# Scores of all attention heads as 64-row products, and the first gate and up weight splits pinned behind the heads, in a two-layer hybrid decoder trunk

## Chip, core and metric

One core of a Trainium2 chip runs the whole program. The metric is the time of one execution in microseconds; the kernel before has a median of 1226.44 us over three runs. Engines are named as in the profile: PE is the matrix engine (PEld its weight loads), DVE, ACT and POOL are the vector, scalar and GpSimd engines, SP issues most of the transfers.

## What is computed

Two layers, each on 512 tokens of width 1024, all in float32. The first half of a layer mixes tokens with two groups of heads; the second half is a gated feed-forward network (hidden width 2816). Cut to what matters:

```python
h = rms_norm(x, attn_pre_g[l]); proj = h @ w_in[l]
# 4 differential heads: two score maps of 64 features each, rotary on a quarter of them
logits = einsum('bqhmd,bkhmd->bhmqk', qi, k) * scale           # m = 0, 1
p = softmax(where(causal, logits, NEG_INF)); p = p[:, :, 0] - lam * p[:, :, 1]
oa = rms_norm(einsum('bhqk,bkhe->bqhe', p, v), diff_sub_g[l]) * (1.0 - lam_init)
# 8 forgetting heads: one score map of 64 features, and a bias from cumulated log gates
logits = einsum('bqhd,bkhd->bhqk', qi, k) * scale + decay
ob = einsum('bhqk,bkhd->bqhd', softmax(where(causal, logits, NEG_INF)), v)
x = x + rms_norm(concat(oa, ob) @ w_out[l], attn_post_g[l])
h = rms_norm(x, ffn_pre_g[l])
x = x + rms_norm((silu(h @ w_gate[l]) * (h @ w_up[l])) @ w_down[l], ffn_post_g[l])
```

## The kernel before

Every float32 operand is split into a high and a low part of a reduced type (a cast on ACT, then a subtraction on DVE or POOL), and a product is the sum of three products: high by high, low by high, high by low. `hT_h` and `hT_l` hold the normed activations, transposed, in the two parts; a weight tile comes through `load_w` (L255) into a raw buffer `wr` and is split into `wh` and `wl`.

**Order.** The head part of a layer (projections, 12 heads, most of the output projection) is written as operations with durations, dependences and slots (`Plan`, L58). The planner walks a simulated clock and emits the instructions of each engine in the order that it finds; `keep_in_program_order` then pins them. PE's fillers are the projections `pj_kd`, `pj_qd`, `pj_kf`, `pj_qf` and the values `vb`, in steps of three products, later the output projection `o`; scores, transposes and value products of the heads go between them. What is not pinned (`load_w` of the feed-forward part) is placed by the framework's scheduler, which may put it among the pinned instructions of ACT and DVE. Each engine works strictly in the order so found.

**Scores.** `tile_chunk` (L693) makes the queries (`q`) or keys (`k`) of 128 features: two maps of a differential head, or two forgetting heads. Its function `stack` gives each of the two 64-feature halves its own full-height operand of 128 rows: for queries the high part in 64 rows and the low part in the other 64; for keys, per half, a high tile and a low tile, each written into 64 rows and then copied to the other 64 by a transfer (`dup`, L742). With 128 rows a single product then sums two of the three terms, so `score` (L880) needs two products per block: stacked queries by the high keys, and by the low keys. Scores land in PSUM banks of tag `s`, of which there are two (`bank_s`). `i` counts the four blocks of 128 queries; block `i` needs `(i+1)*128` key columns. Names in the profile: `sd` and `sf` are the score banks of differential and forgetting heads, `qsd`, `ksd`, `qsf`, `ksf` the operands, `ptd` and `ptf` the transposed probabilities, `od` and `of` the value products, `mixf` the mixed outputs, `pq` a small transpose of the cumulated gates.

**First feed-forward weights.** `gate(0)`, `up(0)` and `gate(f1)` (L1257 and L1260, through `proj_T`) are called after the heads, and their splits are not pinned.

Of the kernel before, what the change touches and what calls it, by code (L numbers as in the profile page):

```python
# [11 lines left out]
F32 = mybir.dt.float32  # L12
# [5 lines left out]
P = 128  # L18
S = 512
# [51 lines left out]
class Plan:  # L71
# [112 lines left out]
def hymba_block(ctx, tc, x_d, pos_d, apre_d, win_d, fb_d, lq1_d, lk1_d, lq2_d, lk2_d, dsg_d, wout_d, apost_d,  # L184
# [67 lines left out]
    G.memset(halfpi, math.pi / 2)  # L252


    def load_w(src, shape, name, eng=None, dst=None, raw=None):  # L255
        n = int(np.prod(shape[1:]))

        def t(tag, dt):
            w = wpool.tile([P, WCH], dt, name=f"{tag}_{name}", tag=tag)[:, :n]
            return w.rearrange("p (a b) -> p a b", a=shape[1])  # L260
        if raw is None:
            w = wpool.tile([P, WCH], F32, name=f"wr_{name}", tag="wr", bufs=NRAW)[:, :n]
            raw = w.rearrange("p (a b) -> p a b", a=shape[1])
        hi, lo = dst or (t("wh", F32R), t("wl", F32R))
        nc.sync.dma_start(raw, src)
        A.copy(hi, raw)  # L266
        (eng or V).tensor_sub(lo, raw, hi.bitcast(F32))  # L267
        return hi, lo

    def split(hi, lo, src):  # L270
# [54 lines left out]
            if store:  # L325
                nc.sync.dma_start(out_d[t * P:(t + 1) * P, c], xs[:, t, c])

    def proj_T(src_w, col, name):

        wh, wl = load_w(src_w[:, col:col + P].rearrange("(k p) n -> p k n", p=P), [P, KT, P], name)  # L330
        ps = bank_g(f"pj_{name}")

        def part(c=slice(0, S), ks=range(KT)):
            for k in ks:
                mm(ps[:, c], wh[:, k], hT_h[:, k, c], k == 0, False)
                mm(ps[:, c], wh[:, k], hT_l[:, k, c], False, False)
                mm(ps[:, c], wl[:, k], hT_h[:, k, c], False, k == KT - 1)
        return ps, part
# [16 lines left out]
    for l in range(DEPTH):  # L355
        win = win_d[l]
        with ExitStack() as actx:
# [339 lines left out]
            def tile_chunk(kind, z, which):  # L697

                need = 8 * z if kind == "d" else 32 + 8 * z
                col = {"dq": QA, "dk": KA, "fq": QB, "fk": KB}[kind + which] + z * P  # L700
                name = f"{which}{kind}{l}{z}"
                box, ready = load(win[:, col:col + P].rearrange("(k p) n -> p k n", p=P), [P, KT, P], name,
                                  eng=V if kind == "d" and l == z == 0 else G)
                b = {}

                def piece(k):
                    def fn():
                        if k == 0:
                            b["ps"] = bank_g(f"pj_{name}")
                        w = box["w"]  # L710
                        mm(b["ps"], w[0][:, k], hT_h[:, k], k == 0, False)
                        mm(b["ps"], w[0][:, k], hT_l[:, k], False, False)
                        mm(b["ps"], w[1][:, k], hT_h[:, k], False, k == KT - 1)
                    return fn
                last_tile[:] = fillers([(650, piece(k)) for k in range(KT)], [ready], take={0: ["g"]}, give=["w"],
                                       key=FILLER - 40 if kind == "d" and l == z == 0 else FILLER)
                done = last_tile[-1]
                key = need - AHEAD_T
                tag = "qs" if which == "q" else "ks"

                def stack(src, deps, give, eng):
                    E = {"V": V, "G": G}[eng]

                    def hi(m):
                        def fn():
                            if m == 0:
                                b["x"] = (q_tile if which == "q" else k_tile)(f"{which}s{kind}{z}")
                            r = HALF[m]
                            return A.copy(b["x"][r, m] if which == "q" else b["x"][r, m, 0], src()[r])
                        return fn  # L730

                    def lo(m):
                        def fn():
                            r, o = HALF[m], HALF[1 - m]
                            x = b["x"]
                            if which == "q":
                                return E.tensor_sub(x[o, m], src()[r], x[r, m].bitcast(F32))
                            return E.tensor_sub(x[r, m, 1], src()[r], x[r, m, 0].bitcast(F32))
                        return fn

                    def dup(m):
                        return lambda: nc.sync.dma_start(b["x"][HALF[1 - m], m].bitcast(F32),  # L742
                                                         b["x"][HALF[m], m].bitcast(F32))
                    ends = []
                    for m in range(2):
                        a = add("A", dA(S), hi(m), deps, key=key, take=[] if m else [tag], order="" if m else tag)
                        d = dV(S) if eng == "V" else dG(S)
                        e = add(eng, d, lo(m), [a], key=key, give=give if m else [], port=kind == "d")
                        if which == "k":
                            e = add("Q", 730, dup(m), [e], key=key, lat=2000)  # L750
                        ends.append(e)
                    qk[(kind, z, which)] = (b, ends)

                if kind == "f":
                    stack(lambda: b["ps"], [done], ["g"], "V")
# [19 lines left out]
                stack(lambda: b["t1"], [g1], ["rc"], "V")  # L775

            vf, vdone = {}, {}
            c_dram = dpool.tile([NFOX, S], F32, name=f"cdram{l}", tag="cdram")
# [102 lines left out]
            def score(kind, h, i, m, n_key, bias=None, pair=None):  # L881
# [8 lines left out]

                def mms():
                    b["s"] = bank_s(f"s{name}")
                    q, ks = qb["x"][:, half, i * P:n], kb["x"]
                    mm(b["s"][:, :n], q, ks[:, half, 0, :n], True, False)
                    mm(b["s"][:, :n], q, ks[:, half, 1, :n], False, True)

                def top():
                    if bias:
# [16 lines left out]
                give = []  # L915
                if i == NT - 1 and (m == 1 if kind == "d" else h % 2):
                    give = ["qs", "ks"]
                o = add("P", n / 1.2 + 5 + PEX / 2, mms, q_ends + k_ends + st["score"] + (bias["op"] if bias else []),
                        key=n_key, take=["s"] if bias else ["s", "e"], give=give)
                st["score"] = [o]  # L920
                v = add("V", dV(n)+80, top, [o], key=n_key, give=["s"])
                return b, add("A", 370 + 0.87 * n, expo, [v], key=n_key)

            def probs(kind, h, i, e_of, deps, key):

# [40 lines left out]
            def diff_head(h, n0):  # L966
                hd = heads.setdefault(("d", h), {"T": []})
                for i in range(NT):
                    n = (i + 1) * P
                    l2 = {}  # L970
                    x = [score("d", h, i, m, n0 + 2 * i + m, pair=l2) for m in range(2)]
                    key = n0 + 2 * i + 1
                    b = {}

# [212 lines left out]
            o1_chunks()  # L1187
            cv = [conv(k, 100) for k in (6, 7)]
            plan.run(tc.keep_in_program_order, first)

            def o0_last(t):
                for k in (6, 7):
# [33 lines left out]
        with ExitStack() as fctx:  # L1226
# [28 lines left out]
                    nc.sync.dma_start(t_d[x, f * P:(f + 1) * P], t)  # L1255

            def gate(f):  # L1257
                return proj_T(wg_d[l], f * P, f"g{l}{f}")

            def up(f):  # L1260
                return proj_T(wu_d[l], f * P, f"u{l}{f}")

            first = {}

# [207 lines left out]
```

## Time and profile before

| what | value |
|---|---|
| median of three runs (lowest, highest) | 1226.44 us (1226.29, 1489.4) |
| the profiled execution, its own time | 1230.15 us |
| its span in the trace | 1228.4 us |
| PE busy, PEld busy | 97 %, 81 % of the span |
| DVE, ACT, POOL busy | 66 %, 49 %, 16 % |
| mean granted clock of PE | 0.987 |

Busy time of an engine is the union of its instructions. PE's products overlap, so a step is read from one start to the next. The page divides the span into 40 slices of 30.7 us; slices 2 to 8 and 21 to 28 hold the head parts of the two layers. The chain of work that ended last is 86 % PE.

### The profile page before, as it was taken

How to read it: one execution, taken by the hardware profiler on the slowest of the kernel's cores; microseconds unless marked ns; L12 is line 12 of the kernel's file. 1: busy time of each engine (PE TensorE's matmuls, PEld its weight loads, DVE VectorE, ACT ScalarE, POOL GpSimd, SP SyncE). 2: the span in 40 equal slices, each digit the busy share in tenths (PEclk: the TensorE clock that was granted, in tenths of full speed). 3: DMA queues.
4: the chain of work that ended last, by engine and by line, in shares of the span. 5: the costliest groups of instructions: out<-in, count | busy, mean ns of one | idle time of the engine just before them, and what ended most of it. 6: DMA issues, size and time to landing. Idle time of an engine off the chain costs nothing.

```text
span 1228.4 us, 16747 instructions
## 1 busy us (share of the span) xinstructions
PE 1196.9 (97%) x5826; PEld 995.6 (81%) x5826; DVE 808.9 (66%) x1588; ACT 598.4 (49%) x1164; POOL 198.6 (16%) x243
## 2 busy tenths in 40 slices
PE   8999999999999999999999899998999999999997
PEld 5888988798888888888778789876988888888886
DVE  6788868565555545577839777784655555455776
ACT  6467767453233232465535768663532332324653
POOL 1213456120000000000231215560200000000010
PEclk9999999999999999999999899998999999999999
DMA  6334444216766757798413333442167667677964
GB/s 217 95 96 117 108 121 136 88 53 201 223 210 208 230 183 234 242 306 301 129 52 89 101 86 88 130 146 69 53 201 225 208 205 230 186 241 235 315 232 138
DMA packets 210884, 206.54 MB, mean 168 GB/s; under 512 B 11360, under 2 KB 155360, under 8 KB 210800
## 3 DMA queue, kind: packets, MB, share of 16 engines
q1 hardware_dynamic: 210128, 204.95, 53.5%
q8 instruction: 46, 0.75, 0.3%
q10 hardware_dynamic: 672, 0.53, 0.1%
q14 instruction: 38, 0.31, 0.1%
HBM read 163.20 MB, written 33.85 MB: 160 GB/s over the span
## 4 chain that ended last, share of the span: by engine, by line
PE 86%; issue 5%; DVE 4%; POOL 2%; DMA 1%; ACT 1%; POOLq 0%; DVEq 0%; SPq 0%
PE pj_g L214 20%; PE pj_u L214 20%; PE o L214 5%; PE da L214 5%; PE dc L214 5%; PE pj_kd L214 4%; PE vb L214 4%; PE pj_qd L214 4%; PE pj_kf L214 4%; PE pj_qf L214 3%; PE va L214 3%; PE db L214 2%; PE sd L214 2%; PE of L214 1%; PE od L214 1%
## 5 line engine op out<-in xcount | busy, mean ns | idle before, releaser
L214 PE MATMUL pj_g<-hT_h,wh_g 128*128 128x512 f32 (+1 forms) x384 | 142.9, 372 | 0.0
L214 PE MATMUL pj_g<-hT_l,wh_g 128*128 128x512 f32 (+1 forms) x384 | 142.7, 372 | 0.0
L214 PE MATMUL pj_g<-hT_h,wl_g 128*128 128x512 f32 (+1 forms) x384 | 142.6, 371 | 0.0
L214 PE MATMUL pj_u<-hT_h,wh_u 128*128 128x512 f32 (+1 forms) x368 | 140.1, 381 | 0.0
L214 PE MATMUL pj_u<-hT_l,wh_u 128*128 128x512 f32 (+1 forms) x368 | 139.8, 380 | 0.0
L214 PE MATMUL pj_u<-hT_h,wl_u 128*128 128x512 f32 (+1 forms) x368 | 139.7, 380 | 0.0
L266 ACT CAST wh_g<-wr_g 128x1024 fp32r<-128x1024 f32 x44 | 46.4, 1054 | 153.1 <-PE pj_u L214 92.3
L267 DVE TENSOR_TENSOR wl_u<-wr_u,wh_u 128x1024 fp32r<-128x1024 f32 x44 | 53.9, 1225 | 94.5 <-ACT wh_u L266 94.5
L279 POOL TENSOR_SCALAR v_fp<-s_fp 128x1 f32<-128x1 f32 x8 | 7.6, 946 | 664.1 <-DVE c L1398 624.9
L266 ACT CAST wh_u<-wr_u 128x1024 fp32r<-128x1024 f32 x44 | 46.3, 1052 | 133.2 <-PE pj_g L214 128.8
L1268 DVE TENSOR_TENSOR sg<-pj_u,sg 128x512 f32<-128x512 f32 x44 | 30.4, 691 | 85.6 <-PE pj_u L214 85.6
L214 PEld LDWEIGHTS pj_g<-hT_h,wh_g 128*128 128x128 f32 x384 | 72.4, 188 | 12.7
L214 PE MATMUL da<-wh_d,op 128*128 128x512 f32 x264 | 82.6, 390 | 0.0
L214 PEld LDWEIGHTS pj_g<-hT_h,wl_g 128*128 128x128 f32 x384 | 72.2, 188 | 12.5
L214 PEld LDWEIGHTS pj_g<-hT_l,wh_g 128*128 128x128 f32 x384 | 72.3, 188 | 12.4
L214 PEld LDWEIGHTS pj_u<-hT_h,wl_u 128*128 128x128 f32 x368 | 69.2, 188 | 13.1
L214 PEld LDWEIGHTS pj_u<-hT_h,wh_u 128*128 128x128 f32 x368 | 69.1, 188 | 13.1
L214 PEld LDWEIGHTS pj_u<-hT_l,wh_u 128*128 128x128 f32 x368 | 69.2, 188 | 12.9
L266 ACT CAST wh_d<-wr_d 128x1024 fp32r<-128x1024 f32 x42 | 44.2, 1052 | 43.3 <-PE da L214 10.7
L267 DVE TENSOR_TENSOR wl_d<-wr_d,wh_d 128x1024 fp32r<-128x1024 f32 x42 | 51.3, 1220 | 15.3 <-ACT wh_d L266 15.2
L266 ACT CAST wh_d<-xr 128x1024 fp32r<-128x1024 f32 (+1 forms) x42 | 38.2, 908 | 42.2 <-PE da L214 12.5
L214 PEld LDWEIGHTS da<-wh_d,op 128*128 128x128 f32 x264 | 49.6, 188 | 10.3
(293 smaller groups left out, 3089.2 us busy)
## 6 DMA issues: line engine op xcount, KB each, us to landing
wr_g<-in_w_gate_dram SPq DMA_DIRECT2D x44, 512.0 KB, 4.5
wr_u<-in_w_up_dram SPq DMA_DIRECT2D x44, 512.0 KB, 4.1
b<-in_w_down_dram SPq DMA_DIRECT2D x88, 256.0 KB, 3.6
t_d<-b SPq DMA_DIRECT2D x88, 256.0 KB, 4.2
wr_d<-t_d SPq DMA_DIRECT2D x24, 512.0 KB, 4.8
wr_d<-in_w_down_dram SPq DMA_DIRECT2D x18, 512.0 KB, 5.0
wr_o<-in_w_out_dram SPq DMA_DIRECT2D x16, 512.0 KB, 3.7
xr<-t_d SPq DMA_DIRECT2D x16, 512.0 KB, 5.1
```

What stands on the lines that cost most here:

```text
L214: ins = PE.matmul(out, a, b, start=start, stop=stop)
L266: A.copy(hi, raw)
L267: (eng or V).tensor_sub(lo, raw, hi.bitcast(F32))
L279: G.tensor_scalar(v, s2[:, 0:1], scalar1=s2[:, 1:2], scalar2=EPS, op0=ALU.add, op1=ALU.add)
L1268: V.tensor_mul(sg, pu, sg)
```

## The change

The high and low parts of queries and keys are no longer stacked into 128 rows. `parts_of` takes the place of `stack`: one cast and one subtraction over all 128 rows, into a high and a low tile; no copies. A score then multiplies 64 rows by 64 rows, in three products. For a differential head, `score_pair` emits the products of its two maps in turn, one on rows 0 to 63, the other on rows 64 to 127, with both `s` banks taken at once; a forgetting head emits its three products on one and the same half. The planner's durations for the scores follow. Apart from that, the splits of the first gate and the first up tile are called right behind the planned part and pinned there. The diff, cut:

```diff
-    def load_w(src, shape, name, eng=None, dst=None, raw=None):
+    def load_w(src, shape, name, eng=None, dst=None, raw=None, pin=False):
...
-        A.copy(hi, raw)
-        (eng or V).tensor_sub(lo, raw, hi.bitcast(F32))
+        for ins in (A.copy(hi, raw), (eng or V).tensor_sub(lo, raw, hi.bitcast(F32))):
+            if pin:
+                tc.keep_in_program_order(ins)
...
+    def feature_w(src_w, col, name, pin=False):
+        return load_w(src_w[:, col:col + P].rearrange("(k p) n -> p k n", p=P), [P, KT, P], name, pin=pin)
+
+    def proj_T(src_w, col, name, w=None):
+
+        wh, wl = w or feature_w(src_w, col, name)
...
-                def stack(src, deps, give, eng):
...
-                            return A.copy(b["x"][r, m] if which == "q" else b["x"][r, m, 0], src()[r])
...
-                            if which == "q":
-                                return E.tensor_sub(x[o, m], src()[r], x[r, m].bitcast(F32))
-                            return E.tensor_sub(x[r, m, 1], src()[r], x[r, m, 0].bitcast(F32))
...
-                        return lambda: nc.sync.dma_start(b["x"][HALF[1 - m], m].bitcast(F32),
-                                                         b["x"][HALF[m], m].bitcast(F32))
...
+                def parts_of(src, deps, give):
+
+                    def hi():
+                        x = (q_tile if which == "q" else k_tile)(f"{which}s{kind}{z}")
+                        b["x"] = x if which == "q" else x[:, 0]
+                        return A.copy(b["x"][:, 0], src())
+
+                    def lo():
+                        return V.tensor_sub(b["x"][:, 1], src(), b["x"][:, 0].bitcast(F32))
...
-                    q, ks = qb["x"][:, half, i * P:n], kb["x"]
-                    mm(b["s"][:, :n], q, ks[:, half, 0, :n], True, False)
-                    mm(b["s"][:, :n], q, ks[:, half, 1, :n], False, True)
+                    r = HALF[half]
+                    for y, (qx, kx) in enumerate(((0, 0), (0, 1), (1, 0))):
+                        mm(b["s"][:, :n], qb["x"][r, qx, i * P:n], kb["x"][r, kx, :n], y == 0, y == 2)
...
-                o = add("P", n / 1.2 + 5 + PEX / 2, mms, q_ends + k_ends + st["score"] + (bias["op"] if bias else []),
+                o = add("P", n / 0.8 + 8 + PEX / 2, mms, q_ends + k_ends + st["score"] + (bias["op"] if bias else []),
...
+            def score_pair(h, i, n_key, l2):
...
+                    for m in range(2):
+                        bs[m]["s"] = bank_s(f"sd{l}{h}{i}{m}")
+                    for z, (x, y) in enumerate(((0, 0), (0, 1), (1, 0))):
+                        for m, r in enumerate(HALF):
+                            mm(bs[m]["s"][:, :n], qb["x"][r, x, i * P:n], kb["x"][r, y, :n], z == 0, z == 2)
...
+                o = add("P", 1.3 * n + 60, mms, q_ends + k_ends + st["score"], key=n_key, take=["s", "s", "e", "e"],
+                        give=["qs", "ks"] if i == NT - 1 else [])
...
-                    x = [score("d", h, i, m, n0 + 2 * i + m, pair=l2) for m in range(2)]
+                    x = score_pair(h, i, n0 + 2 * i, l2)
...
             plan.run(tc.keep_in_program_order, first)
+            early = [feature_w(x[l], 0, f"{n}{l}0", True) for n, x in (("g", wg_d), ("u", wu_d))]
...
-                return proj_T(wg_d[l], f * P, f"g{l}{f}")
+                return proj_T(wg_d[l], f * P, f"g{l}{f}", None if f else early[0])
...
-                return proj_T(wu_d[l], f * P, f"u{l}{f}")
+                return proj_T(wu_d[l], f * P, f"u{l}{f}", None if f else early[1])
```

What PE does at the first scores of a forgetting head in layer 0: before, two products per block on 128 rows.

```order
L214 MATMUL vb_1549<-wh_vb_0_1325,hT_l 128x256
L214 MATMUL sd_1568<-ksd_0_1313,qsd_0_1394 128x512 x2
L219 MATMUL ptd_1573<-con,ed_1454 128x128 x2
L214 MATMUL sf_1576<-ksf_0_1425,qsf_0_1506 128x128 x2
L214 MATMUL vb_1549<-wh_vb_0_1325,hT_h 128x256
```

After the change, three on 64 rows; the blocks are still enclosed by 128-row work (`vb` are values, `ptd` transposes).

```order
L214 MATMUL vb_1560<-wh_vb_0_1361,hT_l 128x256
L214 MATMUL sf_1578<-ksf_0_1423,qsf_0_1511 128x128 x3
L214 MATMUL sf_1584<-ksf_0_1423,qsf_0_1511 128x256 x3
L219 MATMUL ptd_1595<-con,ed_1473 128x128 x2
L214 MATMUL vb_1560<-wh_vb_0_1361,hT_h 128x256
```

The width shown (128x256) is that of the result: queries by keys. Between 128-row products there now stand short runs of 64-row products.

At the first differential head PE had, per block, two products for each of the two maps (bank by bank), with filler steps around them.

```order
L214 MATMUL pj_kd_569<-hT_h,wl_kd_467 128x512
L214 MATMUL sd_592<-ksd_0_503,qsd_0_553 128x256 x2
L214 MATMUL sd_596<-ksd_0_503,qsd_0_553 128x256 x2
L214 MATMUL pj_kd_569<-hT_h,wh_kd_466 128x512
L214 MATMUL pj_kd_569<-hT_l,wh_kd_466 128x512
```

Now the products of a block alternate between the two banks, that is between rows 0 to 63 and rows 64 to 127.

```order
L214 MATMUL pj_kd_571<-hT_l,wh_kd_466 128x512
L214 MATMUL pj_kd_571<-hT_h,wl_kd_467 128x512
L214 MATMUL sd_588<-ksd_0_503,qsd_0_543 128x256
L214 MATMUL sd_589<-ksd_0_503,qsd_0_543 128x256
L214 MATMUL sd_588<-ksd_0_503,qsd_0_543 128x256
```

The alternation goes on to six products; then the filler returns. In the whole changed program the 384 score products stand in 81 such unbroken runs, 30 that begin with a differential head and 51 with a forgetting one.

On ACT, at the end of the heads of layer 0, the splits of the first gate and up tile stood among the exponentials (`ae`) and the casts of the probabilities (`pthf`).

```order
L914 ACTIVATE ae_2623,lf_2664<-ae_2623,mf_2658 128x256
L266 CAST wh_g_3067<-wr_g_3066 128x1024
L914 ACTIVATE ae_2635,lf_2682<-ae_2635,mf_2670 128x384
L1090 COPY mixf_1886<-of_2672 64x512
L947 CAST pthf_2692<-ptf_2694 128x128
L266 CAST wh_u_3074<-wr_u_3073 128x1024
L1098 CAST hT_h<-mixf_1886 128x512
```

Now both stand behind the last cast of the heads, ahead of the squares for the norm (`junk`).

```order
L971 CAST pthf_2747<-ptf_2793 128x384
L1114 COPY mixf_1904<-of_2811 64x512
L1122 CAST hT_h<-mixf_1904 128x512
L266 CAST wh_g_2847<-wr_g_2846 128x1024
L266 CAST wh_u_2853<-wr_u_2852 128x1024
L286 ACTIVATE junk_2869,s_ap_2868<-o_2438 128x512
```

No instruction of a head is queued behind them any more. On SP the transfers of the two raw tiles now stand ahead of those of the two gains of the norms (`g_apost`, `g_fpre`), where they stood behind them.

## Rows read from the trace of the kernel before

**Rows 1.** The page: busy time of engines, then the granted clock in 40 slices.

```profile
PE 1196.9 (97%) x5826; PEld 995.6 (81%) x5826; DVE 808.9 (66%) x1588; ACT 598.4 (49%) x1164; POOL 198.6 (16%) x243
...
PEclk9999999999999999999999899998999999999999
```

**Rows 2.** Windows of both head parts: length, busy (instructions) of PE, PEld, DVE, ACT, POOL, clock, DMA.

```profile
42.00:260.00 218.00, 214.78 (x1163) 180.61 (x1162) 171.06 (x447) 147.19 (x346) 82.23 (x95) 0.99 0.37 105
636.00:875.00 239.00, 225.36 (x1175) 188.47 (x1176) 177.97 (x455) 147.13 (x347) 82.45 (x97) 0.96 0.34 98
```

**Rows 3.** Windows at half clock within the head parts, same columns.

```profile
223.60:227.03 3.43, 3.43 (x12) 2.41 (x11) 2.61 (x7) 1.23 (x5) 0.00 (x0) 0.50 0.66 193
...
838.00:844.84 6.84, 5.99 (x17) 4.51 (x18) 3.07 (x8) 1.10 (x4) 0.00 (x0) 0.50 0.47 136
...
677.60:684.40 6.80, 5.81 (x22) 4.73 (x20) 6.70 (x19) 2.93 (x8) 0.00 (x0) 0.50 0.16 33
...
701.50:708.30 6.80, 6.18 (x17) 5.04 (x18) 4.03 (x15) 4.76 (x18) 0.00 (x0) 0.50 0.28 77
```

**Rows 4.** Timeline, ACT, both ends of heads: start, length, instruction, [idle before <-releaser].

```profile
219.47 1.05 ACT L266 CAST wh_g<-wr_g 128x1024 fp32r<-128x1024 f32 x1 [2.02 <-DMA wr_g<-in_w_gate_dram]
...
832.94 1.05 ACT L266 CAST wh_g<-wr_g 128x1024 fp32r<-128x1024 f32 x1 [3.42 <-DMA wr_g<-in_w_gate_dram]
```

**Rows 5.** Timeline, PE, at the same two places.

```profile
222.55 0.87 PE L219 MATMUL ptf<-con,ae 128*128 128x128 f32 x5 [1.80 <-DVE mixf L1092]
...
837.12 0.66 PE L219 MATMUL ptf<-con,ae 128*128 128x128 f32 x4 [3.56 <-DVE mixf L1092]
838.85 0.48 PE L219 MATMUL ptf<-con,ae 128*128 128x128 f32 x1 [1.07 <-DVE ptlf L951]
```

**Rows 6.** Timeline, PE, scores of the first differential head and what follows them.

```profile
52.98 0.63 PE L214 MATMUL sd<-ksd,qsd 128*128 128x256 f32 x4
53.45 0.39 PE L214 MATMUL pj_kd<-hT_h,wh_kd 128*128 128x512 f32 x1
...
57.51 0.62 PE L214 MATMUL sd<-ksd,qsd 128*128 128x512 f32 x2
57.97 0.40 PE L214 MATMUL pj_kd<-hT_h,wh_kd 128*128 128x512 f32 x1
```

**Rows 7.** Timeline, all engines, where four 8-row products stand between 128-row ones.

```profile
109.06 0.40 PE L214 MATMUL pj_qd<-hT_h,wl_qd 128*128 128x512 f32 x1
...
109.39 0.32 PEld L219 LDWEIGHTS pq<-con,cT 8*128 8x128 f32 x4 [0.36 <-issue]
109.39 0.41 PE L219 MATMUL pq<-con,cT 8*128 8x8 f32 x4
...
109.73 0.50 PE L214 MATMUL pj_qd<-hT_h,wh_qd 128*128 128x512 f32 x1
109.84 0.19 PEld L214 LDWEIGHTS pj_qd<-hT_l,wh_qd 128*128 128x128 f32 x1
...
110.07 0.40 PE L214 MATMUL pj_qd<-hT_l,wh_qd 128*128 128x512 f32 x1
```

**Rows 8.** The tile cT: its instructions, durations min/median/max in ns, first and last start.

```profile
L219 PEld LDWEIGHTS pq<-con,cT x8: 135/136/138, 109.4 to 718.6; 8*128 8x128 f32 x8
...
L865 DVE COPY cT<-pc x2: 660/662/664, 107.3 to 716.3; 8x512 f32<-8x512 f32 x2
```

**Rows 9.** Timeline, PEld, where 128-column weights give way to 64-column ones.

```profile
191.23 0.78 PEld L214 LDWEIGHTS of<-ptlf,vf 128*64 128x64 f32 x4
```

**Rows 10.** Lines by form: one of four groups of half casts (ACT) and half subtractions (DVE).

```profile
L738 DVE TENSOR_TENSOR ksf<-pj_kf,ksf 64x512 fp32r<-64x512 f32 x16 | 11.0, 689 | 6.1 <-ACT ksf L729 5.8
...
L729 ACT CAST ksf<-pj_kf 64x512 fp32r<-64x512 f32 x16 | 9.3, 580 | 0.2
```

**Rows 11.** Timeline, DVE and PE, around the first transposes after the output projection in layer 0.

```profile
246.41 1.42 DVE L294 SCALAR_TENSOR_TENSOR h_f<-xs,r_f,g_fpre 128x512 f32<-128x512 f32 x2 [2.00 <-POOL r_f L280]
...
247.80 0.60 PE L219 MATMUL hp_f<-con,h_f 128*128 128x128 f32 x4
```

More of the change, by code (lines that the diff above doesn't have):

```diff
@@ L326, in post_norm @@
                 nc.sync.dma_start(out_d[t * P:(t + 1) * P, c], xs[:, t, c])
-    def proj_T(src_w, col, name):
-        wh, wl = load_w(src_w[:, col:col + P].rearrange("(k p) n -> p k n", p=P), [P, KT, P], name)
+    def feature_w(src_w, col, name, pin=False):
+        return load_w(src_w[:, col:col + P].rearrange("(k p) n -> p k n", p=P), [P, KT, P], name, pin=pin)
+    def proj_T(src_w, col, name, w=None):
+        wh, wl = w or feature_w(src_w, col, name)
         ps = bank_g(f"pj_{name}")
@@ L719, in tile_chunk @@
                 tag = "qs" if which == "q" else "ks"
-                def stack(src, deps, give, eng):
[L722 to L728, printed above, removed]
-                            return A.copy(b["x"][r, m] if which == "q" else b["x"][r, m, 0], src()[r])
[L730 to L735, printed above, removed]
-                            if which == "q":
-                                return E.tensor_sub(x[o, m], src()[r], x[r, m].bitcast(F32))
-                            return E.tensor_sub(x[r, m, 1], src()[r], x[r, m, 0].bitcast(F32))
-                        return fn
-                    def dup(m):
-                        return lambda: nc.sync.dma_start(b["x"][HALF[1 - m], m].bitcast(F32),
-                                                         b["x"][HALF[m], m].bitcast(F32))
[L744 to L752, printed above, removed]
@@ new lines, in parts_of @@
+                def parts_of(src, deps, give):
[5 more added lines that the diff above has]
+                        return V.tensor_sub(b["x"][:, 1], src(), b["x"][:, 0].bitcast(F32))
+                    a = add("A", dA(S), hi, deps, key=key, take=[tag], order=tag)
+                    qk[(kind, z, which)] = (b, [add("V", dV(S), lo, [a], key=key, give=give, port=True)])
@@ L754, in tile_chunk @@
                 if kind == "f":
-                    stack(lambda: b["ps"], [done], ["g"], "V")
+                    parts_of(lambda: b["ps"], [done], ["g"])
                     return
@@ L774, in tile_chunk @@
                 g1 = add("V", dV(S), t3, [v3], key=key, give=["rd"], port=True)
-                stack(lambda: b["t1"], [g1], ["rc"], "V")
+                parts_of(lambda: b["t1"], [g1], ["rc"])
             vf, vdone = {}, {}
@@ L922, in score, with mms, top, fn @@
                 return b, add("A", 370 + 0.87 * n, expo, [v], key=n_key)
+            def score_pair(h, i, n_key, l2):
+                n = (i + 1) * P
+                (qb, q_ends), (kb, k_ends) = (qk[("d", h, x)] for x in "qk")
+                bs = [{}, {}]
+                def mms():
+                    for m in range(2):
[3 more added lines that the diff above has]
+                            mm(bs[m]["s"][:, :n], qb["x"][r, x, i * P:n], kb["x"][r, y, :n], z == 0, z == 2)
+                def top(m):
+                    def fn():
+                        b = bs[m]
+                        b["e"], b["m"] = half_tile(f"ed{l}{h}{i}{m}"), spool.tile([P, 1], F32, name=f"md{l}{h}{i}{m}",
+                                                                                tag="m")
+                        return V.tensor_tensor_reduce(out=b["e"][:, :n], in0=b["s"][:, :n], in1=mask[:, S - n:],
+                                                      scale=-0.125, scalar=3.0e38, op0=ALU.add, op1=ALU.min,
+                                                      accum_out=b["m"])
+                    return fn
+                def expo(m):
+                    def fn():
+                        b = bs[m]
+                        if m == 0:
+                            l2["l"] = spool.tile([P, 2], F32, name=f"ld{l}{h}{i}", tag="ls2")
+                        e = b["e"][:, :n]
+                        return A.activation(e, e, AF.Exp, bias=b["m"], scale=-1.0, accum_out=l2["l"][:, m:m + 1])
+                    return fn
+                o = add("P", 1.3 * n + 60, mms, q_ends + k_ends + st["score"], key=n_key, take=["s", "s", "e", "e"],
+                        give=["qs", "ks"] if i == NT - 1 else [])
+                st["score"] = [o]
+                ends, last = [], []
+                for m in range(2):
+                    v = add("V", dV(n) + 80, top(m), [o], key=n_key + m, give=["s"])
+                    last = [add("A", 370 + 0.87 * n, expo(m), [v] + last, key=n_key + m)]
+                    ends.append((bs[m], last[0]))
+                return ends
             def probs(kind, h, i, e_of, deps, key):
```

## The prediction

> **What bounds the kernel now.** I read the page first: PE is busy 97 % of the span, no other engine above 66 % [rows 1]. So a change pays or costs by what it does to PE's stream of products and to PE's waits. The windows of the two head parts say how much waiting there is: PE is idle 218.00 - 214.78 = 3.2 us in layer 0 and 239.00 - 225.36 = 13.6 us in layer 1 [rows 2], 16.9 us together. The granted clock is the second loss. It is at its upper level (2.4 GHz) but for four stretches in these parts, where it is 0.50 (1.2 GHz) and PE was busy 3.43 + 5.99 + 5.81 + 6.18 = 21.4 us [rows 3]; at full clock that work takes half, so 10.7 us are lost. Each stretch stands next to a wait of PE. All in all 27.6 us of the head parts are not products at full speed. That is the most that a cure of waits can bring.
>
> Two waits are of one kind. The split of the first gate tile stands on ACT among the exponentials, and ACT sits there until the weights land, 2.02 us in layer 0 and 3.42 us in layer 1 [rows 4]. Heads queue behind it; PE then waits 1.80 us, and 3.56 + 1.07 us [rows 5], and two of the four half-clock stretches follow (223.60 and 838.00) [rows 3].
>
> **The pins, gain 11.1 us.** Behind the last cast of the heads nothing of a head can wait for these weights. That returns 1.80 + 3.56 + 1.07 = 6.4 us of waits and (3.43 + 5.99) / 2 = 4.7 us of half clock. What is queued behind the two casts now is the chain of squares and norms: 2 x 1.05 us of ACT [rows 4] and two subtractions on DVE. The first transpose starts 247.80 - 246.41 = 1.4 us after the two norm products begin, 0.7 us after the first of them is done [rows 11]; ACT and DVE idle around the first squares, so I put the delay at nothing. Without that cover it costs 2.1 - 0.7 = 1.4 us a layer. The gains are queued on SP behind the two raw tiles now. The gate tile was there at 219.47 us, 27 us ahead of the norm products [rows 4, 11]: time enough for them, cost nothing.
>
> **Fewer casts, subtractions and copies.** Of 64 half casts (580 ns in this group) and 64 half subtractions (689 ns) [rows 10] half remain, each over twice the rows and as many columns, which takes no longer. ACT saves 32 x 0.58 = 19 us, DVE 32 x 0.69 = 22 us, over two layers. Both are idle some 20 to 40 % of the head parts [rows 2], so nothing of that is on PE's path by itself; it only shortens waits. The 32 copies of keys leave SP. No wait of PE is put down to them: nothing by itself.
>
> **More products.** A pass over the four blocks of a head costs, in steps from start to start: 256 columns (53.45 - 52.98) / 4 = 0.12, 512 columns (57.97 - 57.51) / 2 = 0.23 [rows 6], 384 halfway, 0.175, and 128 columns no less than a load of weights, which holds back the next load by 109.84 - 109.73 = 0.11 [rows 7]. Sum 0.63 us. 16 forgetting heads go from two passes to three on the same rows: + 16 x 0.63 = 10.1 us. A differential head had four passes (two maps), 2.52 us. Now it has three double passes. If the halves run side by side but the two loads one after the other, a double block costs at least 0.22 (0.23 at 512 columns): 0.89 a pass, 2.67 a head, + 1.2 us for 8 heads. If loads overlap too, 3 x 0.63 = 1.89, - 5.0 us; if nothing overlaps, 6 x 0.63 = 3.78, + 10.1 us. No row shows two halves at once; I take + 1.2, the middle, because loads of weights follow each other in every row here.
>
> **Going into 64 rows and out again.** The trace has one place per layer where products of few rows stand between 128-row ones: `pq`, 8 rows. There PEld is idle 0.36 us with nothing to wait for ("issue"), and the load of `pq` starts 0.33 us after the product ahead of it, not with it; its data had been ready since 108.0 us [rows 7, 8]. On the way back the load comes late again, and the product behind it lasts 0.50 in place of 0.40 us. From 109.06 to 110.07 us there are two products of 512 columns (0.46) and four small ones, whose loads take (0.32 - 0.136) / 3 = 0.06 a step [rows 7, 8], 0.25. That leaves 1.01 - 0.71 = 0.30 us for one visit. A score has a longer first load (0.19 against 0.136), in the open: 0.35. By pieces (0.10 and 0.11 on the way in, 0.07 and 0.11 on the way out) it is 0.39. Where it is the columns that shrink, nothing of this shows: the loads of `of`, 64 columns, have no idle time before them [rows 9]. So the price of 64 rows lies between nothing (like 64 columns) and 0.39 us (like 8 rows); I take 0.35, since it is rows that shrink here too. 81 runs x 0.35 = 28.4 us, at most 31.6.
>
> The Trainium skill, "TensorEngine Tiling (Array Packing)", section "Key Properties", says that changing the tiling mode, not just the tile, drains the engine, without a price. The rows agree for fewer rows and not for fewer columns; by the rule taken alone every one of the 81 runs pays twice, and the sum stays as it is.
>
> **Waits that go along.** Of the 27.6 us the pins take 11.1. The other 16.5 are waits for DVE and ACT in layer 1. PE becomes about 20 us a layer slower between them, while ACT and DVE have 10 us less to do each; so PE comes later to what they make. Between nothing and 16.5 I take 10. A differential pair needs both score banks free, which makes new waits; they are in that choice.
>
> **Sum.** 28.4 + 10.1 + 1.2 - 11.1 - 10 = + 18.6 us on the execution's own 1230.15, 1248.8. That execution was 3.7 us above the median; on the median's scale 1245, 1.5 % slower. With all waits gone and 0.30 a visit it is 1234; with 0.39 and only a quarter of the other waits gone, 1262. That is the forecast's own range.
>
> **Rivals.**
> 1. *64 rows switch for nothing*, as 64 columns do [rows 9]. Then 28.4 us fall away: 1217. With the halves' loads side by side, 1210; with every wait gone as well, 1204. For it: nothing in the rows shows a 64-row product at all. Against it: `pq` in both layers. Chance 0.27.
> The Trainium skill, "TensorE: Matmul & The Clock Gate", part "Packing small matmuls", has matmuls on different rows run concurrently, which is the 1210 case; no run before shows it.
> 2. *The halves of a pair take turns.* Six passes a differential head, + 10.1 in place of + 1.2: 1254. It decides together with a visit at 0.35. For it: strict order of products in every row. Chance 0.13.
> 3. *The clock falls in the heads*, the other side. Place: the runs of scores, where PE now pauses 81 times. Half clock has come beside waits so far [rows 3, 5]; but beside the lone visit of `pq` there is none [rows 3, 7], so one pause doesn't do it. Price: a stretch of 3.43 us costs 1.7. Four of them take the forecast past 1251; if one run in four brings one, 20 x 1.7 = 34 us, 1279. Chance 0.12.
>
> **Chances and range.** Forecast 0.45, rivals 0.27, 0.13, 0.12, the rest (all gains, no price, below 1204) 0.03. The range 1210 to 1264 leaves out some of rival 1 (0.05), rival 3 and the rest: 0.2. A difference under 2 % (1201.9 to 1251.0) is what I count as no change, about what a measurement of this kernel tells apart. Slower: a third of the forecast (0.16), most of rival 2 (0.10), rival 3 (0.12): 0.38. Faster: 0.04. Same: 0.58.
>
> **What would show it.** In the changed profile the first load of each run of `sd` or `sf` should start about 0.33 us after the product ahead of it, with PEld idle before it for "issue", and the product behind the run should last 0.50 us; if the load starts with the product ahead, rival 1 holds. Starts of the two halves of a pair: some 0.11 us apart with 0.22 to the next (forecast), nearly equal (loads overlap), or a full step apart (rival 2). The casts `wh_g`, `wh_u` behind the heads should have no DMA before them, PE no wait for `mixf` of 1.8 or 3.6 us. More half-clock stretches than two within the heads would be rival 3. The feed-forward parts should take the same time as before; a change there is a step that I have missed.

## The result: 1.5 % slower, and the profile after

The changed kernel takes 1245.36 us (median of 4 runs, 1244.17 to 1246.58); the kernel before took 1226.44 us on the same occasion (median of three; a fourth run of it, 1489.4 us, was far slower and is left out). The ratio is 1.0149, with a 95 % interval of 1.0129 to 1.0169: slower beyond noise, but by less than the 2 % that the prediction counts as a change. The profiled run took 1244.17 us, its span is 1242.4 us.

The page after: busy time of the engines and the granted clock in 40 slices, to be held against [rows 1].

```profile
PE 1219.4 (98%) x5954; PEld 993.4 (80%) x5954; DVE 789.0 (64%) x1556; ACT 579.8 (47%) x1132; POOL 200.3 (16%) x243
...
PEclk9999999999999999999999999999999999999999
```

DVE and ACT lost 20 and 19 us of work (22 and 19 were computed). PE gained 22.5 us of busy time, and the dip of its clock in the second head part is nearly gone.

To compare stages between kernels I cut each span at the first `pj_kd` product and the first `hp_f` transpose of a layer. Windows of the kernel before (length, then busy time and instructions of PE, PEld, DVE, ACT, POOL, clock, DMA share, GB/s), the two head parts and the two parts behind them:

```profile
31.88:247.80 215.92, 212.70 (x1144) 178.80 (x1142) 166.90 (x439) 141.02 (x328) 81.23 (x90) 0.99 0.39 108
636.42:862.25 225.83, 212.61 (x1107) 177.71 (x1107) 166.78 (x438) 139.37 (x326) 78.85 (x90) 0.95 0.36 101
247.80:636.42 388.62, 385.87 (x1793) 320.78 (x1791) 233.96 (x335) 157.56 (x249) 20.50 (x29) 1.00 0.63 201
862.25:1228.40 366.15, 358.59 (x1665) 299.64 (x1663) 218.71 (x313) 139.08 (x214) 12.38 (x19) 0.99 0.65 207
```

The same four of the changed kernel, and the one stretch at half clock within its heads:

```profile
31.60:260.72 229.12, 226.88 (x1207) 179.75 (x1206) 156.43 (x423) 131.68 (x312) 81.02 (x90) 1.00 0.28 84
649.00:876.28 227.28, 222.35 (x1170) 175.92 (x1171) 157.68 (x422) 130.03 (x310) 80.76 (x90) 0.98 0.27 82
260.72:649.00 388.28, 385.55 (x1793) 320.69 (x1791) 234.39 (x335) 157.69 (x249) 20.24 (x29) 1.00 0.63 201
876.28:1242.40 366.12, 358.60 (x1665) 299.73 (x1663) 217.93 (x313) 139.08 (x214) 12.34 (x19) 1.00 0.64 207
710.98:717.81 6.83, 6.51 (x20) 4.93 (x21) 3.60 (x15) 3.62 (x13) 0.00 (x0) 0.50 0.28 78
```

The parts behind the heads differ by 0.3 us and less: all of the change is in the heads, 441.75 us before and 456.40 us after. There, three numbers say where it went. **Idle** is length less PE's busy time: 3.22 + 13.22 = 16.44 us before, 2.24 + 4.93 = 7.17 us after. **Half clock** costs half of the busy time in such stretches: 10.7 us before [rows 3], 6.51 / 2 = 3.25 us after. The rest, **work at full clock**, is 441.75 - 16.44 - 10.7 = 414.6 us before and 456.40 - 7.17 - 3.25 = 446.0 us after. So losses, idle and half clock together, fell from 27.1 to 10.4 us, by 16.7 us, and work rose by 31.4 us.

Where the work grew is seen at the first differential head, start and length of each instruction, PE and its weight loads, and the DVE operation that the profile names for the idle time (to be held against [rows 6, 7]):

```profile
51.74 0.69 DVE L401 TENSOR_TENSOR vdl<-va,vdh 128x512 fp32r<-128x512 f32 x1
...
52.47 0.40 PE L214 MATMUL pj_kd<-hT_h,wl_kd 128*128 128x512 f32 x1
...
52.79 0.41 PEld L214 LDWEIGHTS sd<-ksd,qsd 64*128 64x128 f32 x6 [0.36 <-DVE vdl L401]
52.79 0.62 PE L214 MATMUL sd<-ksd,qsd 64*128 64x256 f32 x6
53.34 0.19 PEld L214 LDWEIGHTS pj_kd<-hT_h,wh_kd 128*128 128x128 f32 x1
53.34 0.50 PE L214 MATMUL pj_kd<-hT_h,wh_kd 128*128 128x512 f32 x1
...
53.68 0.40 PE L214 MATMUL pj_kd<-hT_l,wh_kd 128*128 128x512 f32 x1
```

The load of the first 64-row tile starts 0.32 us after the product ahead of it (52.47 to 52.79), and the profile puts its idle time down to `vdl`. But `vdl` had been ready since 52.43, and the scores don't read it. Behind the run the next product lasts 0.50 us in place of 0.40. That is the picture of `pq` [rows 7] once more, and it stands at the runs of scores all over the heads: 31 of the 81 runs follow a product of 512 columns, and in each of these the first load starts 0.32 to 0.33 us behind it.

The splits of the first gate and up tile, on ACT:

```profile
248.35 1.05 ACT L266 CAST wh_g<-wr_g 128x1024 fp32r<-128x1024 f32 x1
249.31 1.05 ACT L266 CAST wh_u<-wr_u 128x1024 fp32r<-128x1024 f32 x1
...
252.73 0.60 ACT L286 ACTIVATE junk<-o 128x512 f32<-128x512 f32 x1 [2.38 <-PE o L214]
...
863.92 1.05 ACT L266 CAST wh_g<-wr_g 128x1024 fp32r<-128x1024 f32 x1
```

No DMA ends an idle time before them, where 2.02 and 3.42 us stood [rows 4], and the squares behind them still wait for PE, not for the casts: the pins delay nothing.

### The profile page after: what moved, and what is told of

The parts are those of the page before. It is cut to its first block, busy times and chain, and to the rows that moved or that the text cites. A ratio compares the mean times of both kernels' runs of the same rounds, so it can differ in the third digit from the quotient of the medians.

```text
span 1242.4 us, 16818 instructions
## 1 busy us (share of the span) xinstructions
PE 1219.4 (98%) x5954; PEld 993.4 (80%) x5954; DVE 789.0 (64%) x1556; ACT 579.8 (47%) x1132; POOL 200.3 (16%) x243
## 4 chain that ended last, share of the span: by engine, by line
PE 90%; issue 5%; DVE 2%; POOL 1%; ACT 1%; DMA 1%; SPq 0%; DVEq 0%; POOLq 0%; ACTq 0%
PE pj_g L214 19%; PE pj_u L214 19%; PE o L214 7%; PE da L214 5%; PE dc L214 5%; PE vb L214 4%; PE pj_kf L214 4%; PE pj_qf L214 4%; PE pj_qd L214 4%; PE pj_kd L214 4%; PE sf L214 3%; PE va L214 3%; PE db L214 2%; PE sd L214 2%; PE of L214 2%
## 5 line engine op out<-in xcount | busy, mean ns | idle before, releaser
L214 PEld LDWEIGHTS pj_g<-hT_h,wl_g 128*128 128x128 f32 x384 | 72.3, 188 | 12.3
```

## The experiments

For each kernel I give the edit, what was expected, the median with its ratio to the kernel before on the same occasion, and where it helps the numbers of the heads, taken as above from the profiled run (loss is idle and half clock together; the kernel before: 27.1 us of loss, 414.6 of work). Several expectations reckon with 0.40 us a visit to 64 rows, an estimate; the price measured below is lower.

### The change taken apart

**Pins alone.** The kernel before with the pins of the diff and nothing else. It ran twice.

```diff
+            early = [feature_w(x[l], 0, f"{n}{l}0", True) for n, x in (("g", wg_d), ("u", wu_d))]
...
-                return proj_T(wg_d[l], f * P, f"g{l}{f}")
+                return proj_T(wg_d[l], f * P, f"g{l}{f}", None if f else early[0])
```

> The kernel before with the pinned splits alone; scores stay stacked on 128 rows. Theory (pins give back 6.4 us of waits and 4.7 us of half clock): 11 us less than before, about 1216, PE without the waits of 1.80 and 3.56 us for mixf at the end of the heads, and two half-clock stretches fewer. Rival (the waits were only covering others, or the splits now delay the norm chain): within 4 us of before.

> The kernel before with the pinned splits alone, once more, beside the two others on the same chip. Both theories: 1216 to 1220.

Measured 1217.87 us, 0.9913 [0.9893, 0.9934], and the second time 1217.53 us, 0.9923 [0.9907, 0.9938]. Head parts of the first, and its stretches at half clock:

```profile
31.64:245.36 213.72, 211.29 (x1143) 177.77 (x1143) 166.92 (x439) 141.23 (x328) 81.13 (x90) 1.00 0.38 109
634.78:852.66 217.88, 209.29 (x1107) 175.86 (x1107) 166.65 (x438) 139.12 (x326) 78.61 (x90) 0.97 0.37 105
675.78:682.61 6.83, 5.96 (x22) 4.88 (x22) 6.73 (x19) 2.93 (x8) 0.00 (x0) 0.50 0.15 31
699.68:706.50 6.82, 6.11 (x17) 4.97 (x18) 4.05 (x14) 4.78 (x18) 0.00 (x0) 0.50 0.28 79
```

The two half-clock stretches behind the `mixf` waits are gone, the other two stay. Loss 2.4 + 8.6 + (5.96 + 6.11) / 2 = 17.1 us, 10.1 less than before; work 414.5, unchanged. In the profile of the second run the stretch at 675.78 is missing too: loss 14.0 us, 13.1 less than before, at 415.2 of work. So the loss differs by some 3 us between executions of one kernel, the work by less than 1. The medians fell by 9.0 and 9.7 us. The term of 11.1 us was right for the pins by themselves, as far as these executions agree.

**64 rows without the pins.** The changed kernel with the pins taken out.

```diff
-            early = [feature_w(x[l], 0, f"{n}{l}0", True) for n, x in (("g", wg_d), ("u", wu_d))]
...
-                return proj_T(wg_d[l], f * P, f"g{l}{f}", None if f else early[0])
+                return proj_T(wg_d[l], f * P, f"g{l}{f}")
```

> The changed kernel without the pins. Theory (the switches in and out of 64 rows cost 81 x 0.40 = 32 us, third passes 10, pairs -5, and fewer waits elsewhere): slower than the changed kernel by what the pins are worth beside it, up to 11 us, so 1249 to 1256. Rival (the pins carry nothing once PE is slower): 1245, like the changed kernel.

Measured 1248.14 us, 1.0164 [1.0147, 1.0180]. That is just below the expected 1249 to 1256. Beside the scores of 64 rows the pins are worth 1248.1 - 1245.4 = 2.8 us, not 9. By the ratios it is 1.8 us: the two kernels ran on different occasions, and the intervals of their ratios overlap. Loss is 12.3 us without them and 10.4 with them. PE has no wait for `mixf` of over 0.2 us here, though nothing is pinned. On ACT, at the first gate tile of layer 1:

```profile
854.42 1.05 ACT L266 CAST wh_g<-wr_g 128x1024 fp32r<-128x1024 f32 x1 [0.82 <-DMA wr_g<-in_w_gate_dram]
```

The cast waits for the weights 0.82 us in place of 3.42 [rows 4]. SP issues the transfer about 20 us later in the span (848.87 us in place of 828.94), and so does ACT come to the cast, but now 4.7 us behind the issue in place of 0.6. That fits slower scores, which give the transfer more time; the order of ACT has changed as well, and the two were not taken apart. That more work of PE alone hides such waits is seen in the control with 128 rows below: its edit is an added product and nothing else, its waits for `mixf` are 2.0 us in place of 5.4, and its loss is 22.1 us in place of 27.1.

**Pairs of the differential heads alone**, with the pins; the forgetting heads keep their stacked operands and two products.

```diff
-                    parts_of(lambda: b["ps"], [done], ["g"])
+                    stack(lambda: b["ps"], [done], ["g"], "V")
...
-                    for y, (qx, kx) in enumerate(((0, 0), (0, 1), (1, 0))):
-                        mm(b["s"][:, :n], qb["x"][r, qx, i * P:n], kb["x"][r, kx, :n], y == 0, y == 2)
+                    mm(b["s"][:, :n], q, ks[:, half, 0, :n], True, False)
+                    mm(b["s"][:, :n], q, ks[:, half, 1, :n], False, True)
```

> Pins, and 64-row pairs for differential heads only; forgetting heads stacked on 128 rows with copies, as before. Theory: 30 runs x 0.40 = 12 us for the switches, -5 us for the halves side by side, from the 1216 of the pins alone: 1221 to 1225, near the kernel before. Rival (the forgetting heads' third pass isn't what costs, the pairs are): 1235 or more.

Measured 1219.62 us, 0.9932 [0.9915, 0.9948]. That is under the expected 1221 to 1225. Loss 11.2 us, work 420.0, 5.4 more than before.

**Forgetting heads alone**, with the pins; the differential heads keep `stack` and two products, map by map.

```diff
-                parts_of(lambda: b["t1"], [g1], ["rc"])
+                stack(lambda: b["t1"], [g1], ["rc"], "V")
...
-                    x = score_pair(h, i, n0 + 2 * i, l2)
+                    x = [score("d", h, i, m, n0 + 2 * i + m, pair=l2) for m in range(2)]
```

> Pins, and 64-row scores for forgetting heads only; differential heads stacked as before. Theory: 51 runs x 0.40 = 20 us and 10 us of third passes on top of the 1216 of the pins alone, less some waits: 1238 to 1246. Rival (forgetting heads in 64 rows are cheap): below 1228.

Measured 1240.10 us, 1.0100 [1.0082, 1.0118]. Loss 10.6 us, work 441.4, 26.8 more than before. So the forgetting heads make the kernel slow: of the 31.4 us of added work some 26.8 are theirs, some 5.4 the pairs'.

### The price of a visit to 64 rows

Into the kernel before I put one more product of 128 key columns in front of each of the 128 pairs of stacked products. The next product overwrites it, so nothing of the computation changes. Three kernels differ in the shape of that product alone: 64 rows, 128 rows as the control, and 128 rows by 64 columns.

```diff
+                    mm(b["s"][:, :P], qb["x"][:HD, half, i * P:n], ks[:HD, half, 0, :P], True, True)
                     mm(b["s"][:, :n], q, ks[:, half, 0, :n], True, False)
```

> The kernel before with one more product in front of each of the 128 score groups, on 64 rows, 128 columns of keys, into the group's own bank, where the next product overwrites it. Theory (each visit to 64 rows costs 0.40 us beside its own product of 0.12): up to 128 x 0.52 = 67 us more, 55 to 67 if waits shrink. Rival (64 rows switch for nothing): 128 x 0.12 = 15 us more.

```diff
+                    mm(b["s"][:, :P], q, ks[:, half, 0, :P], True, True)
                     mm(b["s"][:, :n], q, ks[:, half, 0, :n], True, False)
```

> The control: the same extra product on all 128 rows. Both theories: 128 x 0.12 = 15 us more than before, 8 to 16 if waits hide some. The difference to the 64-row kernel is 128 times the price of going in and out: 51 us by the theory, 0 by the rival.

```diff
+                    mm(b["s"][:HD, :P], qb["x"][:, half, i * P:i * P + HD], ks[:, half, 0, :P], True, True)
                     mm(b["s"][:, :n], q, ks[:, half, 0, :n], True, False)
```

> The same extra product on 128 rows with 64 columns of weights. Theory (only a change of rows empties the array): like the 128-row control or a little less, since the load of 64 columns is shorter: 6 to 15 us more than before. Rival (any change of the tiling empties it): 55 to 67 us more.

Measured 1272.43 us (1.0356 [1.0330, 1.0381]), 1239.04 us (1.0082 [1.0055, 1.0109]) and 1240.42 us (1.0091 [1.0063, 1.0120]). The first adds 44.7 us, less than the expected 55 to 67; the other two lie where they were expected. The head parts of the first two kernels, and their stretches at half clock:

```profile
31.75:272.37 240.62, 238.65 (x1207) 189.28 (x1206) 167.96 (x439) 141.67 (x328) 79.52 (x90) 1.00 0.34 97
661.20:905.80 244.60, 235.68 (x1170) 185.66 (x1171) 169.31 (x438) 140.10 (x326) 75.97 (x90) 0.98 0.33 93
731.22:741.46 10.24, 9.07 (x23) 6.50 (x24) 6.80 (x27) 6.57 (x23) 0.00 (x0) 0.50 0.19 51
```

```profile
32.34:258.14 225.80, 221.31 (x1207) 187.67 (x1206) 168.44 (x439) 141.22 (x328) 80.77 (x90) 0.98 0.36 103
646.70:872.31 225.61, 214.24 (x1171) 180.68 (x1172) 169.34 (x438) 139.87 (x326) 78.99 (x90) 0.98 0.36 101
100.33:103.74 3.41, 3.41 (x14) 3.02 (x13) 2.31 (x8) 2.66 (x10) 2.41 (x1) 0.50 0.05 14
233.45:236.86 3.41, 3.41 (x14) 2.82 (x12) 3.07 (x7) 1.06 (x3) 0.00 (x0) 0.50 0.16 41
711.32:718.14 6.82, 5.56 (x17) 4.62 (x18) 3.90 (x13) 4.84 (x19) 0.00 (x0) 0.50 0.28 77
```

Work in the heads, busy time less half of that at half clock, is 238.65 + 235.68 - 9.07 / 2 = 469.8 us, in the same way 429.4 us for the control, and 428.4 us with 64 columns. The control adds 14.8 / 128 = 0.116 us a product, which is the load of weights that the prediction took as its lower bound (0.11). Half the columns cost nothing more than that. Half the rows cost (469.8 - 429.4) / 128 = 0.32 us a visit on top. PE at one place of the kernel with 64 rows:

```profile
53.22 0.40 PE L214 MATMUL pj_kd<-hT_h,wl_kd 128*128 128x512 f32 x1
53.55 1.44 PE L214 MATMUL sd<-ksd,qsd 64*128 64x128 f32 x6
54.83 0.39 PE L214 MATMUL pj_kd<-hT_h,wh_kd 128*128 128x512 f32 x1
```

and of the control at the same place:

```profile
53.46 0.39 PE L214 MATMUL pj_kd<-hT_h,wl_kd 128*128 128x512 f32 x1
53.69 0.87 PE L214 MATMUL sd<-ksd,qsd 128*128 128x128 f32 x6
54.39 0.40 PE L214 MATMUL pj_kd<-hT_h,wh_kd 128*128 128x512 f32 x1
```

From filler product to filler product it is 1.61 us against 0.93. The group of six holds two extra products, thus two visits: 0.34 us each. The first product comes 0.33 us behind the one ahead, against 0.23.

So 64 rows behave like the 8 rows of `pq`, and 64 columns like `of` [rows 7, 9]. The Trainium skill, "TensorEngine Tiling (Array Packing)", section "Key Properties", has a drain at each change of the tiling mode. These runs agree for rows and put 0.32 us on it; for columns they show no such cost.

With 0.32 us a visit the work of each kernel can be added up from its number of runs, 10.1 us for the third passes of the forgetting heads, and -5.0 us for the differential heads if the two halves of a pair overlap fully:

| kernel | sum | measured |
|---|---|---|
| pairs alone, 30 runs | 30 x 0.32 - 5.0 = +4.6 | +5.4 |
| forgetting alone, 52 runs | 52 x 0.32 + 10.1 = +26.7 | +26.8 |
| the changed kernel, 81 runs | 81 x 0.32 + 10.1 - 5.0 = +31.0 | +31.4 |

### Whether the halves of a pair run side by side

The changed kernel with the two loops swapped: three products of the lower half, then three of the upper.

```diff
-                    for z, (x, y) in enumerate(((0, 0), (0, 1), (1, 0))):
-                        for m, r in enumerate(HALF):
+                    for m, r in enumerate(HALF):
+                        for z, (x, y) in enumerate(((0, 0), (0, 1), (1, 0))):
```

> The changed kernel with the six products of a pair in another order: three of the lower half, then three of the upper one. Theory (halves overlap only where they stand next to each other): two pass times in place of one, 8 heads x 3 x 0.63 = 15 us more than the changed kernel, less at the one place where the halves meet: 1255 to 1260. Rival (the order doesn't matter): 1245.

Measured 1245.22 us, 1.0130 [1.0105, 1.0155]: the same time as the changed kernel. The theory, which had a loss here, was wrong: the order within the six doesn't matter. The first loads and products of such a group of six, with the loops swapped:

```profile
57.73 0.19 PEld L214 LDWEIGHTS sd<-ksd,qsd 64*128 64x128 f32 x2 [0.36 <-DVE ptld L975]
57.73 0.50 PE L214 MATMUL sd<-ksd,qsd 64*128 64x512 f32 x2
```

Two loads start within 0.01 us of each other and take 0.19 us together, as one does, and so do two products of 512 columns, which on one half would stand 0.23 us apart. They are the first of each half: the upper half doesn't wait for the three products of the lower one that were written ahead of it. That is the sign that the prediction gave for loads that overlap (starts nearly equal); in the changed kernel it is the same, with two loads and two products at 52.79. Scores in the changed kernel, a group of products to a line: form and count, busy us, mean ns of one, idle before:

```profile
L214 PE MATMUL sf<-ksf,qsf 64*128 64x512 f32 x48 | 15.0, 419 | 0.0
...
L214 PE MATMUL sf<-ksf,qsf 64*128 64x128 f32 x48 | 8.8, 289 | 0.0
L214 PE MATMUL sd<-ksd,qsd 64*128 64x512 f32 x48 | 7.7, 426 | 0.0
...
L214 PE MATMUL sd<-ksd,qsd 64*128 64x128 f32 x48 | 4.4, 289 | 0.0
```

and with the loops swapped:

```profile
L214 PE MATMUL sd<-ksd,qsd 64*128 64x512 f32 x48 | 7.8, 426 | 0.0
...
L214 PE MATMUL sd<-ksd,qsd 64*128 64x128 f32 x48 | 4.5, 290 | 0.0
```

The same 48 products take half the busy time in pairs, at 512 columns as at 128, where a load of weights is all that bounds a product. So the loads of the two halves overlap throughout, in either order. What the six products of 512 columns cost, in the kernel with the loops swapped:

```profile
57.40 0.40 PE L214 MATMUL pj_kd<-hT_h,wl_kd 128*128 128x512 f32 x1
57.73 0.97 PE L214 MATMUL sd<-ksd,qsd 64*128 64x512 f32 x6
58.63 0.50 PE L214 MATMUL pj_kd<-hT_h,wh_kd 128*128 128x512 f32 x1
58.97 0.40 PE L214 MATMUL pj_kd<-hT_l,wh_kd 128*128 128x512 f32 x1
```

From 57.40 to 58.97 are 1.57 us: two fillers (0.46), three passes of 0.23 (0.69) and 0.42 for the visit. Six passes one after the other would be 1.38 without any visit, and the whole run has 1.57 - 0.46 = 1.11. The visit is dearer here, between products of 512 columns, than the mean of 0.32.

### Filling both halves everywhere

If a 64-row run pays only with both halves full, the forgetting heads should go in pairs too: their scores by the same loop as `score_pair`, both heads of a tile at once, 64 runs in place of 81, and a planner's duration that counts the visit.

```diff
-            def fox_head(hh, n0):
+            def fox_pair(g, n0):
...
+                        for z, (x, y) in enumerate(((0, 0), (0, 1), (1, 0))):
+                            for m, r in enumerate(HALF):
+                                mm(bs[m]["s"][:, :n], qb["x"][r, x, i * P:n], kb["x"][r, y, :n], z == 0, z == 2)
```

> The changed kernel with the scores of two forgetting heads emitted together, one on rows 0 to 63, the other on rows 64 to 127, as the two maps of a differential head are; the planner counts a run at 1.3 n + 400 ns. The 384 products then stand in 64 runs, not 81. Theory (two halves cost the time of one, also across heads, and a run costs 0.32 us, as the sums of the runs before give): 17 x 0.32 = 5 us and 16 x 3 x 0.63 / 2 = 15 us less work for PE than in the changed kernel: 1225, up to 1235 if both heads of a pair wait for the same buffers. Rival (only the maps of one head overlap, or waits eat it): 1240 or more.

Measured 1224.44 us, 0.9979 [0.9969, 0.9989]: as expected, 21 us below the changed kernel. Work 424.2 us, 9.6 more than before, where 64 x 0.32 - 5.0 - 5.0 gives 10.5. The forgetting scores now take half the time too:

```profile
L214 PE MATMUL sf<-ksf,qsf 64*128 64x512 f32 x48 | 7.7, 426 | 0.0
```

Against the pins alone (1217.7 us) it is still 6.7 us slower: the stacked products need no visits at all. It lies below the kernel before because its loss is 12.4 us in place of 27.1, with 9.6 us more work. How much of that the pins bring here is not shown: the pairs were not run without them.

**The planner's price.** In pairs alone, the duration of a pair raised to what it takes, to see whether a wrong plan cost the pairs their gain.

```diff
-                o = add("P", 1.3 * n + 60, mms, q_ends + k_ends + st["score"], key=n_key, take=["s", "s", "e", "e"],
+                o = add("P", 1.3 * n + 380, mms, q_ends + k_ends + st["score"], key=n_key, take=["s", "s", "e", "e"],
```

> Pins and 64-row pairs for differential heads alone, as in the run of that name, but the planner now counts a pair at 1.3 n + 380 ns in place of 1.3 n + 60, so that it knows of the switch. Theory (the switch is time of PE itself; a better order can only shorten the 9 us of waits left): 1216 to 1220, like the pins alone. Rival (the planner's wrong price made bad orders): 1212 or less.

Measured 1220.03 us, 0.9944 [0.9926, 0.9962], against 1219.62 without. The plan's number is worth nothing here; the visits are a cost of PE, not of the order.

## Why the prediction was right, and where it was not

The median of 1245.4 us lies next to the forecast of 1245, but that nearness is luck in good part: the terms of added work and of removed losses were off in opposite directions, and the two profiled runs lie on opposite sides of their medians (below). The mechanism, more work of PE against fewer waits, was right.

1. **A visit to 64 rows: right in kind, a little large.** 0.35 us was taken, 0.32 measured. Over 81 runs that is 26 us in place of 28.4. The load comes late as in `pq`, and the product behind lasts 0.50 us, as said. Rival 1 (64 rows switch for nothing) falls: the pairs' and the heads' kernels need the price, and the extra 64-row products show it by themselves.
2. **The third pass of the forgetting heads: right.** 10.1 us in the sum; forgetting alone closes with it to 0.1 us.
3. **The pairs: the wrong one of three values.** The text took + 1.2 us "because loads of weights follow each other in every row here". This step failed: those rows hold full-height loads only. The halves' loads overlap, so the lower bound held, - 5.0 us. This term was 6.2 us too high, the largest miss. Rival 2 (halves take turns) falls with it, and its argument too, since even in turn they overlap.
4. **Pins and other waits: too much gain.** The sum had - 11.1 and - 10, together - 21.1 us; losses fell by 16.7. The pins alone bring 10.1, the 64-row scores alone 27.1 - 12.3 = 14.8, but both together not 24.9: they remove the same waits, those for `mixf` among them, which are gone with either. The prediction named this effect (PE comes later to what the others make) for the other waits and did not apply it to those of the pins.
5. **The new wait for both banks** exists, and stood in the choice for the waits. PE in layer 1, around the start of the half-clock stretch shown above:

```profile
708.30 0.83 PE L214 MATMUL sd<-ksd,qsd 64*128 64x256 f32 x6 [0.45 <-DVE md L925]
...
711.30 1.03 PE L214 MATMUL sd<-ksd,qsd 64*128 64x384 f32 x3 [2.17 <-DVE md L925]
```

   2.6 us of waits, until DVE has read the banks of the block before, and 3.3 us of half clock with them. But at this place of the kernel before PE stood longer, for another reason, and had a stretch of the same length at half clock (701.50 in [rows 3]):

```profile
702.12 0.77 PE L214 MATMUL pj_kd<-hT_h,wh_kd 128*128 128x512 f32 x1 [3.30 <-DVE vf L823]
```

   So the wait for the banks has taken another's place, and no run shows that it made the kernel slower.
6. **Rival 3 (the clock falls in the heads)** is refuted: 81 runs and one stretch in the profiled run, and that one behind a wait. With the loops swapped there are two, of 3.41 us each, both behind waits of PE.
7. **Casts, subtractions and copies: not contradicted.** ACT and DVE got 19 and 20 us shorter, and the table needs work on PE alone. That the copies by themselves are worth nothing was not tried.
8. **The upper end of the forecast's own range doesn't follow from its words.** 0.39 us a visit and a quarter of the other 16.5 us gives 31.6 + 10.1 + 1.2 - 11.1 - 4.1 = + 27.7 us, thus 1254; 1262 comes out only if a quarter of all 27.6 us goes. The measured time lies well inside either.

Together the sum had + 39.7 us of work (28.4 + 10.1 + 1.2) and - 21.1 of losses; measured + 31.4 and - 16.7. The misses of 8.3 and 4.4 us partly cancel, and 0.7 us were saved ahead of the heads and behind them: + 18.6 forecast, + 14.0 between the two profiled runs (1230.15 and 1244.17). That the medians differ by 18.9 comes from the profiled runs, that of before 3.7 us above its median, that of after 1.2 us below. I can't say which waits differ from run to run.

## What to carry to other kernels

Products of half the rows did not pay here even with both halves of the array full: 9.6 us more work than stacked ones. Count the entries and exits, 0.32 us for each visit here, before counting passes, and keep a stacked full-height product where it already does two terms in one. An estimate from these numbers: with both halves full a pair of maps saves 0.63 us of passes and makes four visits, 1.28 us, so runs would have to be about twice as long to break even; that was not tried. Gains of waits do not add: work that makes the bounding engine slower hides the same waits that another edit removes, so measure each part alone. Here the pins alone, at some 1217.7 us, beat both kernels, 0.8 to 0.9 % below the kernel before.

## What the hardware showed that I had not expected

- Two halves of the array load weights and multiply side by side, whichever order the six products stand in: two loads and two products start at 57.73 us though three products of one half were written first, and it takes 7.7 and 7.8 us of busy time for 48 products of 512 columns, against 15.0 us on one half at a time. The Trainium skill, "TensorE: Matmul & The Clock Gate", part "Packing small matmuls", says that matmuls in different tiles of the array run concurrently; the runs agree for halves of the rows.
- Reducing the columns of the weights to 64 cost nothing (428.4 against 429.4 us of work), reducing the rows to 64 cost 0.32 us a visit.
- 81 pauses of some 0.1 us on the way into the runs (0.32 us from start to start in place of 0.23) did not lower the clock: the profile of the changed kernel shows a single stretch at half clock in the heads, at a wait of 2.17 us.
